# The first layer's MLPs end by halves of tokens, and norms over 256 tokens sum their squares on TensorE

## The chip, the cores and the metric

The kernel runs on one core of one Trainium2 chip. The metric is device time in microseconds (us): 2271.27 us is the median of three runs of the kernel before. One further execution was profiled; all rows below come from it.

## The reference, cut to what matters

Two layers over 1024 tokens of 1024 features. Each layer has a mixer (a state-space mixer in the first, attention over selected keys in the second) and then an MLP, and each of the two is wrapped in norms on both sides:

```python
def rms_norm(x, g):
    y = x * rsqrt(mean(x * x, axis=-1, keepdims=True) + 1e-6)
    return y * g

for i in range(2):
    mix = (s5_mixer, dsa_mixer)[i](rms_norm(h, norm_g[i, 0]), ...)
    h = h + rms_norm(mix, norm_g[i, 1])
    ff = relu(rms_norm(h, norm_g[i, 2]) @ w1[i]) ** 2 @ w2[i]     # 1024 -> 4096 -> 1024
    h = h + rms_norm(ff, norm_g[i, 3])
```

Everything is float32. The change is about the end of the MLP of layer 0: its second product, the norm behind it with the residual sum (gain 3 of the kernel), and the norm ahead of the attention of layer 1 (gain 4).

## The kernel before, in words

The tokens are worked in two halves of 512. Features lie on partitions: an activation of one half is four blocks `[128, 2, 512]` (eight parts of 128 features). To keep float32 accuracy each operand of a large product is split into a high and a low part, and `mm3` (L159 to L161) issues three matmuls for one product, each with 128x128 weights and 512 moving columns. The low parts of weights are made by VectorE and GpSimd (L143), the high ones by ScalarE (L142).

`mlp` has 16 `pair`s of units of `w1` and eight steps `c` of `w2`. In a step four units `d` are loaded, and for each unit and each `j` twelve matmuls fill one PSUM tile `m` that VectorE adds to the accumulator `acc` (L341). With `finish` given, the last step is worked otherwise: its four units are kept (tag `wl`), run first for the tokens 0 to 255 and then for 256 to 511 (matmuls with 256 moving columns, VectorE's sum at L326), and `finish` is called after each half. Only the very last MLP of the program (layer 1, second half) does so before the change.

A norm needs, for each token, the sum of squares over eight parts of 128 features. `squares` has ScalarE square the parts (L186 to L189), an engine add them up (VectorE in the norms of this case, L193), and TensorE reduce over the partitions: for 128 tokens at a time the sum of the parts is the weights and a single column of ones is what moves (L196, output `c`, 128x1; the profile counts two for each such float32 matmul). `post_norm` then forms the reciprocal root on VectorE and ScalarE (L234, `rsqrt` at L167 to L171), spreads it over the partitions with transposes on TensorE (L238), copies it (L240, `rb`), multiplies (L252) and adds the residual (L262). `pre_norm` with gain 4 scales and splits its input into the attention's `x1`, and forms its own squares. `att_r` turns the result into tables for the rotation; its transposes on TensorE are L1179, which wait for copies on ScalarE (L1177).

`run` strings this together: MLP of layer 0 over half 0, `post_norm`, store, `pre_norm`, `att_r`; MLP of layer 0 over half 1, with index, projections and the first attention work of half 0 beside it (the generator `first`); then `att_in(0)`, the same two norms over half 1, `att_r(1)`, and the attention's output product and `index(1)`; later layer 1's MLPs. Within these limits a scheduler sets the order in which each engine gets its instructions: behind a norm that waits, TensorE has matmuls of the next stage in the queue, in the order the scheduler wrote.

## Time and profile before

| what | value |
|---|---|
| median of three runs (lowest, highest) | 2271.27 us (2270.70, 2272.05) |
| the profiled execution: its time | 2264.73 us |
| the profiled execution: its span | 2262.6 us |
| mean granted clock of TensorE | 0.978 of full speed |
| TensorE busy | 2153.9 us, 95% of the span |
| VectorE, ScalarE, GpSimd busy | 1428.8, 1083.2 and 706.5 us |

The span runs from the first to the last instruction on the core; the 2.1 us between it and the execution's time lie around the program. The medians' runs were made apart from the profiled one, which was 6.5 us shorter than their median. "Granted clock" is the share of its full speed (2.4 GHz) that TensorE was given in a stretch; 0.50 is the lower of two levels, 1.2 GHz.

### The profile page before, as it was taken

The page shows a single profiled execution, that of the slowest core. Times are in us where ns is not written, and L with a number is a line of the kernel's source. Part 1 is how long each engine was busy: PE and PEld are TensorE (multiplying, and loading weights), DVE is VectorE, ACT ScalarE, POOL GpSimd, SP SyncE. Part 2 cuts the span into 40 slices and gives each one's busy share as a digit, 9 for nine tenths or more (in the row PEclk, how much of TensorE's full clock was granted, in tenths as well). Part 3 has the DMA queues.
Part 4 walks back from the last instruction along what each step waited for, and adds up shares of the span by engine and source line. Part 5 has one row for each costly group of instructions (what it writes and reads, how often), then busy time and mean ns, then how long its engine had stood idle before and what let it go on. Part 6 is the DMA issues. An engine that isn't in the chain of part 4 may idle for free.

```text
span 2262.6 us, 29481 instructions
## 1 busy us (share of the span) xinstructions
PE 2153.9 (95%) x10376; PEld 1778.6 (79%) x10376; DVE 1428.8 (63%) x2756; ACT 1083.2 (48%) x2024; POOL 706.5 (31%) x593
## 2 busy tenths in 40 slices
PE   8998999999989999999988988999999899999997
PEld 4677788888878888888867866888788687888886
DVE  8667943333745687555686889998767477333335
ACT  5436633333543575555463555787456353333332
POOL 1114632222346423222347533222311135222222
PEclk9999999999999999999999999999999999999998
DMA  7113432333437653445446533334222434423231
GB/s 292 30 32 124 160 111 96 100 94 102 131 105 208 154 132 107 117 107 163 143 146 174 163 102 103 96 82 101 79 81 74 144 137 154 147 84 111 85 112 38
DMA packets 115892, 266.81 MB, mean 118 GB/s; under 512 B 14240, under 2 KB 49568, under 8 KB 115744
## 3 DMA queue, kind: packets, MB, share of 16 engines
q1 hardware_dynamic: 101840, 240.77, 33.3%
q0 software_dynamic: 12672, 23.07, 5.4%
q8 instruction: 82, 1.34, 0.3%
q10 hardware_dynamic: 1232, 1.08, 0.1%
q14 instruction: 66, 0.54, 0.1%
HBM read 229.02 MB, written 34.67 MB: 117 GB/s over the span
## 4 chain that ended last, share of the span: by engine, by line
PE 73%; DVE 14%; ACT 5%; issue 5%; POOL 1%; DMA 1%; SPq 0%; DVEq 0%; ACTq 0%; POOLq 0%
PE m L159 17%; PE m L160 17%; PE m L161 17%; PE m L636 2%; PE p L159 2%; PE p L161 2%; PE p L160 2%; PE p L1082 2%; PE p L1062 2%; DVE wh L143 1%; DVE b L252 1%; PE p L1091 1%; PE p L1090 1%; DVE b L209 1%; ACT junk L1000 1%
## 5 line engine op out<-in xcount | busy, mean ns | idle before, releaser
L159 PE MATMUL m<-b,wh 128*128 128x512 f32 (+1 forms) x2208 | 859.9, 392 | 25.0 <-DVE acc L341 11.0
L160 PE MATMUL m<-b,wh 128*128 128x512 f32 (+1 forms) x2208 | 856.6, 390 | 5.1 <-DVE b L209 4.7
L161 PE MATMUL m<-b,wh 128*128 128x512 f32 (+1 forms) x2208 | 855.0, 390 | 4.3 <-DVE wh L143 4.3
L143 POOL TENSOR_TENSOR wh<-wr,wh 128x512 fp32r<-128x512 f32 (+1 forms) x342 | 440.8, 1294 | 1223.7 <-ACT wh L142 1139.8
L142 ACT ACTIVATE wh<-wr 128x512 fp32r<-128x512 f32 (+1 forms) x684 | 395.3, 592 | 502.7 <-PE m L161 416.2
L159 PEld LDWEIGHTS m<-b,wh 128*128 128x128 f32 x2208 | 418.4, 190 | 113.1 <-DVE acc L341 11.6
L161 PEld LDWEIGHTS m<-b,wh 128*128 128x128 f32 x2208 | 418.5, 190 | 89.3 <-DVE wh L143 5.1
L160 PEld LDWEIGHTS m<-b,wh 128*128 128x128 f32 x2208 | 418.8, 190 | 88.3 <-DVE b L209 6.0
L143 DVE TENSOR_TENSOR wh<-wr,wh 128x512 fp32r<-128x512 f32 (+1 forms) x342 | 266.6, 787 | 294.3 <-ACT wh L142 284.1
L341 DVE TENSOR_TENSOR acc<-acc,m 128x512 f32<-128x512 f32 x216 | 147.1, 682 | 154.0 <-PE m L161 152.3
L306 ACT ACTIVATE b<-m 128x512 f32<-128x512 f32 x128 | 76.2, 595 | 163.6 <-PE m L161 160.6
L150 DVE CAST b<-b 128x1024 fp32r<-128x1024 f32 x68 | 58.1, 854 | 126.8 <-ACT b L308 120.5
L161 PE MATMUL p<-b,wh 128*128 128x512 f32 (+1 forms) x304 | 114.6, 387 | 6.7 <-DVE wh L143 6.7
L159 PE MATMUL p<-b,wh 128*128 128x512 f32 (+1 forms) x304 | 112.9, 388 | 3.2 <-ACT b L747 3.2
L160 PE MATMUL p<-b,wh 128*128 128x512 f32 (+1 forms) x304 | 115.9, 386 | 0.0
L1086 ACT ACTIVATE pt<-p 128x512 fp32r<-128x512 f32 (+1 forms) x160 | 83.6, 553 | 65.6 <-PE p L1082 63.2
L1087 DVE TENSOR_TENSOR pt<-p,pt 128x512 fp32r<-128x512 f32 (+1 forms) x160 | 99.0, 630 | 24.5 <-ACT pt L1086 24.3
L1069 ACT ACTIVATE s<-s,ring 128x128 f32<-128x128 f32 (+7 forms) x128 | 98.5, 772 | 31.7 <-DVE ring L1066 31.3
L1000 ACT ACTIVATE junk<-b,ring 128x512 bf16<-128x512 f32 (+2 forms) x90 | 80.6, 896 | 58.4 <-DVE ring L996 51.8
L1062 PE MATMUL p<-kt,q 128*128 128x512 f32 (+2 forms) x384 | 98.5, 363 | 0.0
L1082 PE MATMUL p<-con,s 128*128 128x128 f32 x576 | 93.8, 272 | 0.8 <-DVE ring L1066 0.7
L1066 DVE CUSTOM_DVE_ANT_0 s<-p,nb 128x512 f32<-128x512 f32 (+3 forms) x128 | 72.6, 583 | 32.8 <-PE p L1062 26.7
(314 smaller groups left out, 2738.8 us busy)
## 6 DMA issues: line engine op xcount, KB each, us to landing
wr<-in_w_dram SPq DMA_DIRECT2D x256, 512.0 KB, 3.7
wr<-in_wa_dram SPq DMA_DIRECT2D x32, 512.0 KB, 3.7
q<-qd POOLq DMA_DIRECT2D x64, 256.0 KB, 5.5
ld<-hd SPq DMA_DIRECT2D x24, 512.0 KB, 6.1
hd<-b SPq DMA_DIRECT2D x16, 512.0 KB, 4.6
qd<-b SPq DMA_DIRECT2D x128, 64.0 KB, 2.0
wr<-in_wao_dram SPq DMA_DIRECT2D x16, 512.0 KB, 3.7
q<-qi POOLq DMA_DIRECT2D x24, 256.0 KB, 4.6
```

Source lines behind the costliest of these rows:

```text
L142: nc.scalar.activation(ph, pr, AF.Copy)
L143: (nc.gpsimd if h else nc.vector).tensor_sub(pl, pr, ph.bitcast(F32))
L159: mm(ps, w[0], x[0], start=start, stop=False)
L160: mm(ps, w[0], x[1], start=False, stop=False)
L161: return mm(ps, w[1], x[0], start=False, stop=stop)
L341: nc.vector.tensor_add(acc[d][:, j], acc[d][:, j], ps)
L1000: nc.scalar.activation(junk[:, 1, :W[j]], keys[j].bitcast(F32), AF.Sign, bias=neg[:, j:j + 1], accum_out=cnt[:, j:j + 1])
L1062: nc.tensor.matmul(ps[:, :m], qt[:, v, 2 * hp + k, :], self.K[c][g // 2][:, g % 2, :m], start=v == 0, stop=v == 1)
L1069: nc.scalar.activation(s, s, AF.Exp, bias=least, scale=-1.0, accum_out=self.sums[:, h:h + 1])
L1082: nc.tensor.transpose(pt[:, kk, k, :], P[k][:, (k0 + kk) * 128:(k0 + kk + 1) * 128], self.ident)
L1086: nc.scalar.activation(ph[:, :nk], pt[:, :nk], AF.Copy)
L1087: nc.vector.tensor_sub(pl[:, :nk], pt[:, :nk], ph.bitcast(F32)[:, :nk])
```

## The change

Two things change. `squares` has a second form, used wherever a norm runs over 256 tokens: ScalarE squares each of the eight parts by itself, nothing is added on VectorE, and TensorE accumulates all eight parts in PSUM, eight matmuls with one moving column for each 128 tokens instead of one. And both MLPs of layer 0 get a `finish`: their last step runs by halves of 256 tokens, and after each half the residual is loaded, `post_norm` runs, the result is stored, and `pre_norm` writes its part of `x1` and of `r`. The work beside the MLP is drained ahead of the last step, and `att_in(0)` is called when the first half of the second MLP is done. Norms over 256 tokens are those of the very last MLP too, so these change in their squares alone.

```diff
--- before.py
+++ after.py
@@ -178,7 +178,22 @@
 
     def squares(self, blocks, add):
 
         nc = self.nc
+        if add is None:
+            n = blocks[0].shape[-1] // 128
+            sqs = []
+            for j, b in enumerate(blocks):
+                sq = self.blk([128, 2, 512], tag=self.scratch_tag)[:, :, :128 * n]
+                for q in range(2):
+                    nc.scalar.activation(sq[:, q], b[:, q], AF.Square)
+                    sqs.append(sq[:, q])
+            ps = self.pc()
+            for k, sq in enumerate(sqs):
+                for t in range(n):
+                    nc.tensor.matmul(ps[:, t:t + 1], sq[:, t * 128:(t + 1) * 128], self.ones,
+                                     start=k == 0 and t == 0, stop=k == 7 and t == n - 1)
+            return ps[:, :n]
         acc, n = None, blocks[0].shape[-1]
         for j, b in enumerate(blocks):
             sq = self.blk([128, 2, 512], tag=self.scratch_tag)[:, :, :n]
@@ -196,26 +211,27 @@
             nc.tensor.matmul(ps[:, j:j + 1], acc[:, j * 128:(j + 1) * 128], self.ones, start=True, stop=True)
         return ps[:, :n // 128]
 
-    def pre_norm(self, h, gi, tag="b", square=True):
+    def pre_norm(self, h, gi, tag="b", square=True, into=None):
 
 
         nc = self.nc
         out = []
         for j, b in enumerate(h):
-            hi, lo = [self.blk([128, 2, 512], F32R, tag=tag) for _ in range(2)]
+            hi, lo = into[0][j] if into else [self.blk([128, 2, 512], F32R, tag=tag) for _ in range(2)]
             for q in range(2):
                 g = self.gain[:, gi, 2 * j + q:2 * j + q + 1]
                 nc.scalar.activation(hi[:, q], b[:, q], AF.Copy, scale=g)
                 nc.vector.scalar_tensor_tensor(lo[:, q], b[:, q], g, hi.bitcast(F32)[:, q],
                                                op0=ALU.mult, op1=ALU.subtract)
             out.append((hi, lo))
-        s = self.squares(h, nc.gpsimd.tensor_add if square else nc.vector.tensor_add)
-        r = self.small([128, 4], F32, "kept")
+        s = self.squares(h, None if into else nc.gpsimd.tensor_add if square else nc.vector.tensor_add)
+        r = into[1] if into else self.small([128, 4], F32, "kept")
         nc.vector.tensor_scalar(r, s, 1.0 / 1024, EPS, op0=ALU.mult, op1=ALU.add)
         if square:
             nc.vector.scalar_tensor_tensor(r, r, 1024 * EPS, r, op0=ALU.mult, op1=ALU.mult)
         else:
-            nc.vector.tensor_copy(r, self.rsqrt(r, 4)[:, :4])
+            n = r.shape[-1]
+            nc.vector.tensor_copy(r, self.rsqrt(r, n)[:, :n])
         return out, r
 
     def post_norm(self, f, gi, h, e=None, reorder=False, last=None, aside=False):
@@ -223,8 +239,8 @@
 
 
         nc = self.nc
-        s = self.squares(f, nc.vector.tensor_add)
         n = f[0].shape[-1]
+        s = self.squares(f, nc.vector.tensor_add if n == 512 else None)
         m = n // 128
         ms = self.small([128, 4], F32)
         if e is None:
@@ -314,6 +330,8 @@
             while len(hid) < min(2 * c + 3 + (c >= 6), 16):
                 pair(len(hid))
             if finish and c == 7:
+                for _ in side or ():
+                    pass
                 ws = [self.unit(w2[L, c, d], last=True) for d in range(4)]
                 for th in range(2):
                     n = slice(256 * th, 256 * th + 256)
@@ -1253,9 +1271,32 @@
             self.store_h(dst[hf], h)
             return h
 
+        def halves(hf, first=lambda: None):
+
+
+            x = [tuple(self.blk([128, 2, 512], F32R) for _ in range(2)) for _ in range(4)]
+            r = self.small([128, 4], F32, "kept")
+
+            def take(n, f):
+                if not n.start:
+                    first()
+                m = slice(n.start // 128, n.stop // 128)
+
+                def load(j):
+                    t = self.blk([128, 2, 512], name="ld", tag="ld")[:, :, :256]
+                    self.nc.sync.dma_start(t, hd[0][hf][j][:, :, n])
+                    return t
+
+                h = self.post_norm(f, 3, [lambda j=j: load(j) for j in range(4)], xn[hf][1][:, m])
+                for j in range(4):
+                    self.nc.sync.dma_start(hd[1][hf][j][:, :, n], h[j])
+                self.pre_norm(h, 4, square=False, into=([[t[:, :, n] for t in b] for b in x], r[:, m]))
+
+            return take, x, r
+
         self.nc.sync.dma_start(self.rope, a["rope"])
-        acc = self.mlp(0, xn[0][0])
-        x1, r = self.pre_norm(residual(0, acc, 3, hd[0], hd[1], xn[0][1]), 4, square=False)
+        take, x1, r = halves(0)
+        self.mlp(0, xn[0][0], finish=take)
         self.att_r(0, r)
         self.att_start()
 
@@ -1264,9 +1305,11 @@
             yield from self.projections(0, x1)
             yield from self.attention_a()
 
-        acc = self.mlp(0, xn[1][0], first(), PER_A, WAIT_A)
-        xo = finished(self.att_in(0, "x"))
-        x1, r = self.pre_norm(residual(1, acc, 3, hd[0], hd[1], xn[1][1]), 4, square=False)
+        side = first()
+        xo = []
+        take, xb, r = halves(1, lambda: xo.extend(finished(self.att_in(0, "x"))))
+        self.mlp(0, xn[1][0], side, PER_A, WAIT_A, finish=take)
+        x1 = xb
         self.att_r(1, r)
         for _ in self.att_out(xo, "hid"):
             pass
```

The change moves instructions on TensorE at three places. First, TensorE at the end of the first MLP. `m_530` to `m_570` are tiles of the second MLP's first product, `c_492` (before) is the sum of squares of the post-norm over 512 tokens, `c_516` (after) that of the pre-norm over tokens 0 to 255 and `c_532` that of the post-norm over tokens 256 to 511. Before, one of the two places with one-column matmuls reads:

```order
L159 MATMUL m_530_4299<-b262_1730,wh529_0_4293 128x512
L160 MATMUL m_530_4299<-b263_1731,wh529_0_4293 128x512
L196 MATMUL c_492_4134<-con_72,b488_4118 128x1 x4
L161 MATMUL m_530_4299<-b262_1730,wh529_0_4293 128x512
L159 MATMUL m_530_4299<-b264_1736,wh529_0_4293 128x512
```

and of the change, the longest such row of that place:

```order
L160 MATMUL m_568_4515<-b269_1749,wh567_1_4512 128x512
L194 MATMUL c_516_4218<-con_72,b512_4206 128x1 x4
L194 MATMUL c_516_4218<-con_72,b513_4209 128x1 x4
L194 MATMUL c_516_4218<-con_72,b514_4212 128x1 x4
L194 MATMUL c_516_4218<-con_72,b515_4215 128x1 x4
L194 MATMUL c_532_4366<-con_72,b528_4354 128x1 x4
L194 MATMUL c_532_4366<-con_72,b529_4357 128x1 x4
L194 MATMUL c_532_4366<-con_72,b530_4360 128x1 x4
L194 MATMUL c_532_4366<-con_72,b531_4363 128x1 x4
L161 MATMUL m_568_4515<-b268_1748,wh567_1_4512 128x512
```

Four one-column matmuls stood between two wide ones; now 32 stand there in a row. Two further groups of 16 stand behind the first half of tokens (broken by a single wide matmul) and at the end of the place, and the end of the second MLP has the same three groups.

Second, TensorE at the transposes of `att_r` (`p1_521` and `p1_523` before, `p1_552` after) a little later. Before:

```order
L159 MATMUL m_558_4575<-b538_4400,wh555_1_4557 128x512
L160 MATMUL m_558_4575<-b539_4401,wh555_1_4557 128x512
L161 MATMUL m_558_4575<-b538_4400,wh555_1_4557 128x512
L1179 MATMUL p1_521_4231<-con_72,b522_4232 128x128 x4
L1179 MATMUL p1_523_4239<-con_72,b524_4240 128x128
L159 MATMUL p1_560_4597<-b503_4176,wh559_0_4591 128x512
```

After the change:

```order
L159 MATMUL m_582_4663<-b268_1748,wh581_1_4660 128x512
L160 MATMUL m_582_4663<-b269_1749,wh581_1_4660 128x512
L1197 MATMUL p1_552_4473<-con_72,b553_4474 128x128 x4
L161 MATMUL m_582_4663<-b268_1748,wh581_1_4660 128x512
L159 MATMUL m_584_4697<-b262_1730,wh583_0_4691 128x512
```

The two groups of transposes were adjacent; now the first stands among wide matmuls, and the second group further behind.

Third, TensorE at the end of the program (`m_3116` before, `m_3178` after: the last tile of the last product). Before:

```order
L160 MATMUL m_3116_18785<-b3073_18338,wh3089_1_18514 128x256
L161 MATMUL m_3116_18785<-b3072_18337,wh3089_1_18514 128x256
L196 MATMUL c_3121_18815<-con_72,b3117_18799 128x1 x2
L238 MATMUL c_3126_18824<-con_72,ring_73 128x128 x2
L1381 UNCONDITIONAL_BRANCH
```

After the change:

```order
L161 MATMUL m_3178_19279<-b3134_18821,wh3151_1_18998 128x256
L194 MATMUL c_3183_19305<-con_72,b3179_19293 128x1 x4
L194 MATMUL c_3183_19305<-con_72,b3180_19296 128x1 x4
L194 MATMUL c_3183_19305<-con_72,b3181_19299 128x1 x4
L194 MATMUL c_3183_19305<-con_72,b3182_19302 128x1 x4
L254 MATMUL c_3188_19328<-con_72,ring_73 128x128 x2
```

Sixteen one-column matmuls have taken the place of two behind the last wide one. Apart from the ends of the three MLPs TensorE's order is unchanged.

## Rows read from the trace of the kernel before

**Rows 1.** This is the page: the span's line, and TensorE's line of busy time (us, share of the span, number of instructions); and from its DMA issues the loads of the residual (number, KB each, median us from issue to landing).

```profile
span 2262.6 us, 29481 instructions
...
PE 2153.9 (95%) x10376; PEld 1778.6 (79%) x10376; DVE 1428.8 (63%) x2756; ACT 1083.2 (48%) x2024; POOL 706.5 (31%) x593
...
ld<-hd SPq DMA_DIRECT2D x24, 512.0 KB, 6.1
```

**Rows 2.** This is the timeline of TensorE around 588 us, in the middle of a stretch of 512-column matmuls; columns as in the next groups too: start us, duration us, engine, line, operation, output <- inputs, shape of the moving operand and type, how many, and in brackets idle time before and what ended it. `128x1` is the matmul with one moving column.

```profile
588.06 0.39 PE L160 MATMUL m<-b,wh 128*128 128x512 f32 x1
588.29 0.95 PE L196 MATMUL c<-con,b 128*128 128x1 f32 x8
589.09 0.49 PE L161 MATMUL m<-b,wh 128*128 128x512 f32 x1
589.42 0.40 PE L159 MATMUL m<-b,wh 128*128 128x512 f32 x1
```

**Rows 3.** This is the timeline of TensorE: two 512-column matmuls that are twelve apart in an undisturbed row, and two 256-column matmuls that are twelve apart in the last MLP.

```profile
622.12 0.39 PE L160 MATMUL m<-b,wh 128*128 128x512 f32 x1
...
624.84 0.39 PE L160 MATMUL m<-b,wh 128*128 128x512 f32 x1
...
2239.06 0.28 PE L159 MATMUL m<-b,wh 128*128 128x256 f32 x1
...
2240.50 0.28 PE L159 MATMUL m<-b,wh 128*128 128x256 f32 x1
```

**Rows 4.** This is the waits of TensorE at the end of the first MLP (620 to 650 us; engine, line waited for, us in total, times, longest), and its timeline there.

```profile
PE c L196 <- DVE b L193: 3.8, 1, 3.8
PE p L1179 <- ACT b L1177: 1.9, 1, 1.9
...
630.18 1.84 PE L196 MATMUL c<-con,b 128*128 128x1 f32 x8 [3.82 <-DVE b L193]
```

**Rows 5.** This is busy time by stretch at the same place: from:to us, its length, busy us and (number) of PE, PEld, DVE, ACT and POOL, the granted clock of TensorE, DMA share, GB/s.

```profile
626.00:630.20 4.20, 0.38 (x3) 0.05 (x1) 4.06 (x6) 1.31 (x4) 1.49 (x1) 0.80 0.42 125
630.20:635.35 5.15, 5.15 (x16) 4.47 (x17) 4.67 (x12) 1.49 (x5) 1.42 (x2) 0.50 0.34 105
...
640.10:642.10 2.00, 0.08 (x2) 0.07 (x2) 0.00 (x0) 1.88 (x5) 1.40 (x2) 1.00 0.00 0
642.10:645.55 3.45, 3.45 (x9) 2.80 (x10) 0.00 (x0) 0.00 (x0) 0.00 (x0) 0.51 0.48 152
```

**Rows 6.** This is the waits of TensorE at the end of the second MLP of the first layer (1099 to 1160 us), and its timeline at the first of them.

```profile
PE p L1179 <- ACT b L1177: 2.9, 2, 1.4
PE c L196 <- DVE b L193: 2.0, 1, 2.0
...
1141.54 1.02 PE L196 MATMUL c<-con,b 128*128 128x1 f32 x8 [2.04 <-DVE b L193]
```

**Rows 7.** This is busy time by stretch at that place; columns as in rows 5.

```profile
1139.50:1141.50 2.00, 0.01 (x1) 0.00 (x0) 1.79 (x4) 2.00 (x6) 0.12 (x1) 1.00 0.53 121
1141.50:1143.90 2.40, 2.36 (x14) 2.13 (x15) 2.30 (x3) 2.40 (x7) 1.87 (x2) 1.00 0.29 118
1143.90:1147.30 3.40, 3.40 (x9) 2.65 (x8) 3.37 (x6) 0.52 (x2) 2.12 (x2) 0.50 0.50 152
...
1149.10:1153.10 4.00, 1.11 (x10) 0.88 (x9) 1.49 (x6) 3.25 (x8) 1.41 (x2) 1.00 0.10 39
```

**Rows 8.** This is busy time by stretch at two places of the first mixer, where TensorE runs matmuls with 16 and with 128 moving columns (95.6 and 120.6 us) and 512-column ones behind the second (127.4 us), and at a wait of 1.84 us in a later stage (871.8 us); columns as in rows 5.

```profile
95.60:101.80 6.20, 6.20 (x31) 6.20 (x32) 4.64 (x6) 1.59 (x3) 0.00 (x0) 0.53 0.10 28
...
120.60:127.40 6.80, 6.78 (x31) 6.39 (x32) 5.20 (x6) 0.99 (x2) 0.00 (x0) 0.50 0.00 0
127.40:130.20 2.80, 2.80 (x9) 2.23 (x9) 0.74 (x1) 2.51 (x4) 0.00 (x0) 0.51 0.23 64
...
874.25:877.65 3.40, 3.40 (x10) 2.66 (x9) 3.40 (x9) 0.00 (x0) 1.01 (x1) 0.50 0.33 98
```

**Rows 9.** This is the timeline of TensorE and of VectorE at the end of the program: last wide matmul and squares' matmuls; then VectorE's chain for the reciprocal root, behind the first half of the tokens (2236.52 to 2237.90) and behind the second, and its products and sums.

```profile
2243.82 0.28 PE L161 MATMUL m<-b,wh 128*128 128x256 f32 x1
2246.56 1.01 PE L196 MATMUL c<-con,b 128*128 128x1 f32 x4 [2.46 <-DVE b L193]
...
2236.52 0.16 DVE L234 TENSOR_TENSOR ring<-c,con 128x2 f32<-128x2 f32 x1
...
2237.90 0.16 DVE L171 SCALAR_TENSOR_TENSOR ring<-ring 128x2 f32<-128x2 f32 x1
...
2247.61 0.16 DVE L234 TENSOR_TENSOR ring<-c,con 128x2 f32<-128x2 f32 x1 [1.11 <-PE c L196]
...
2249.18 0.65 DVE L171 SCALAR_TENSOR_TENSOR ring<-ring 128x2 f32<-128x2 f32 x1
2251.09 4.75 DVE L252 SCALAR_TENSOR_TENSOR acc<-acc,con,rb 128x256 f32<-128x256 f32 x8 [1.26 <-ACT rb L240]
2255.76 2.76 DVE L262 TENSOR_TENSOR acc<-acc,ld 128x256 f32<-128x256 f32 x8
```

**Rows 10.** This is busy time by stretch at the end of the program; columns as in rows 5.

```profile
2247.60:2250.00 2.40, 0.03 (x1) 0.06 (x2) 1.84 (x5) 0.20 (x1) 2.40 (x5) 0.50 0.00 0
...
2251.10:2262.60 11.50, 0.00 (x0) 0.00 (x0) 7.41 (x16) 0.00 (x0) 2.47 (x4) 0.50 0.48 163
```

## The prediction

> **What bounds the kernel now.** The page comes first: TensorE is busy for 95% of the span and no other engine for more than 63% [rows 1]. So a microsecond of work put into TensorE's row costs a microsecond unless the row was waiting there, and work taken from VectorE is worth only what TensorE waits for it. I therefore went through TensorE's idle time and its granted clock at the three places where its order changes.
>
> At the end of the first MLP the waits name two things [rows 4]: the one-column matmuls wait 3.82 us for VectorE's sum of squares, and the transposes of `att_r` 1.9 us for a copy on ScalarE. The clock falls to 0.50 with the first wait and to 0.51 with the second, and stays there for 5.15 us and 3.45 us of busy time [rows 5]. At full clock wide matmuls start 0.227 us apart ((624.84 - 622.12) / 12 [rows 3]); at half clock half of the time is lost: 2.6 and 1.7 us. Together 3.8 + 1.9 + 2.6 + 1.7 = 10.0 us.
>
> At the end of the second MLP the same waits are 2.0 and 2.9 us [rows 6], and one low stretch of 3.40 us costs 1.7 us [rows 7]: 6.6 us. At the end of the program [rows 9] nothing runs beside the chain: the last wide matmul starts at 2243.82, the squares' matmuls at 2246.56 after 2.46 us of waiting, VectorE's chain for the root runs from 2247.61 to 2249.83 and the products and sums from 2251.09 to 2258.52.
>
> **The change part by part.** All terms are made against the profiled execution, 2264.7 us; the sum is then laid on the median, 2271.3 us, which stands 6.5 us above it.
>
> *One-column matmuls.* The row at 588 us gives their price inside a busy stretch [rows 2]. The L160 at 588.06 is followed by four of them (eight in the profile's count) and one L161; undisturbed, the L159 would start two spacings after it, at 588.51. It starts at 589.42: 0.91 us for four, 0.227 us each. Nothing hides this, since TensorE was full before and behind. The squares of 512 tokens took 4 per norm; two norms of 256 take 2 x 16. Two norms at each MLP end make 64 instead of 8: 56 x 0.227 = 12.7 us per MLP end. At the program's end 16 for the first half instead of 2 cost 14 x 0.227 = 3.2 us in the busy row; the last 16 run mostly while squares are still being made.
>
> *Narrower matmuls.* The last step has four units of two tiles of twelve: 96 matmuls of 512 columns become 192 of 256. These start 0.120 us apart (1.44 us for twelve [rows 3]), so 96 x (2 x 0.120 - 0.227) = +1.3 us per MLP end.
>
> *The waits that go.* With halves, the first half's norms lie beside the second half's matmuls, and the second half's post-norm has `m` tiles of the next MLP (first place) or `att_in(0)` (second place) in the queue. ScalarE's squares of a part need no sum on VectorE behind them, and the adjacent transposes are apart. What may be late next is the eighth square on ScalarE, whose matmul stands ahead of wide ones in TensorE's queue; I keep 1 us of waits at each place. Gain: 10.0 - 1 = 9.0 and 6.6 - 1 = 5.6 us. The bounds are the whole gain on one side and a wait as long as the old one on the other (rival 2).
>
> *Transfers and order.* The residual now comes in eight loads instead of four at each end, and the result leaves in eight stores, all on SP's queue among the weights' loads. A load there took 6.1 us from issue to landing [rows 1], and the first half's norms have the second half's matmuls beside them (96 x 0.120 = 11.5 us), so I cost them at nothing; without that cover a late load would delay the residual sum, and through it `x1` and the projections. The work beside the second MLP is drained ahead of its last step and `att_in(0)` called within it, but TensorE's order away from the three ends is what it was, so this costs nothing either.
>
> *The end of the program.* VectorE's chain takes 2.2 us behind the second half but only 1.5 us behind the first (2236.52 to 2238.06 [rows 9]); GpSimd was busy for all of the 2.40 us around the slow one [rows 10]. With the sums gone the chain and the products (4.75 + 2.76 us) meet less of it: I take -0.7 for the chain and -1.3 for products and sums; ends of this estimate: 0 and -3. With 0.1 for small things the place is 3.2 + 0.1 - 2.0 = +1.3 us.
>
> Sum at a full clock: (12.7 + 1.3 - 9.0) + (12.7 + 1.3 - 5.6) + 1.3 = 5.0 + 8.4 + 1.3 = **+14.7 us**.
>
> *The clock.* The groups of one-column matmuls are long: 16 take 3.6 us, 32 take 7.3 us. No row of before shows one so long, so the cost has two ends. Below it is nothing, if TensorE's being busy is enough. The rows speak against that: at 95.6 us TensorE was busy for all of 6.20 us with matmuls of few columns at a clock of 0.53, at 120.6 us for 6.78 of 6.80 at 0.50, and the clock came back only after 2.8 us of 512-column matmuls [rows 8]. And at 1139.5 us a wait of 2.04 us and eight one-column passes together were followed by a low clock [rows 6, 7], where the transposes' waits of up to 1.4 us (1149 us) were not. Above, the clock falls soon after a group begins, and a one-column pass then takes twice as long (eight in 1.84 us at 630.18 against 0.95 at 588.29 [rows 2, 4]). For the 32 I let the clock fall after 2 to 4 us: the remaining 3.3 to 5.3 us double, and the 3.4 us of wide matmuls at half clock behind them [rows 7, 8] lose 1.7: 5.0 to 7.0, taken as 5.5 us. The 16 fall only late in the group or not at all: 0 to 3.5, taken as 2 us each. Per MLP end 2 + 5.5 + 2 = 9.5 us, twice 19; at the program's end 2 us for its first group. Clock: **+21.0 us**, nearest to the rows of 95.6 and 120.6 us.
>
> For the clock's other end there is a page: the Trainium skill, "TensorE: Matmul & The Clock Gate", section "Why this matters for your kernels", has it that the clock is lost through idle gaps between bursts of matmuls. By that alone the groups cost nothing for the clock, and the sum would be +14.7 us. The rows at 95.6 us do not settle this, because they show a clock that does not rise, not one that falls in busy time.
>
> Total: 14.7 + 21.0 = +35.7 us: 2264.7 + 35.7 = 2300.4 us profiled, and 2271.3 + 35.7 = **2307 us** for the median.
>
> **The rivals.**
> 1. *The clock holds.* Long one-column groups count as work for the clock like wide ones. Then 2271.3 + 14.7 = 2286 us. For it: no row shows a fall without a wait ahead. Against: the low clock through busy stretches of small matmuls.
> 2. *The waits stay.* ScalarE makes 16 squares of 256 tokens for each half's two norms, besides the splits of weights (L142). If it is behind, TensorE waits at the groups as long as it did for VectorE, 3.8 and 2.0 us, and for transposes 1.9 and 2.9: 10.6 us in all, 2 of which are in the sum: 2307 + 8.6 = 2316 us.
> 3. *The passes are cheap (the other sign).* At one place, the norms' groups: were the one-column matmuls hidden behind wide ones, 126 of them (56 + 56 + 14) would cost none of their 28.6 us, the clock would have no long stretch to fall in, and 14.7 - 28.6 = -13.9 gives 2257 us. It becomes a gain when a matmul costs under 0.227 - 14.7 / 126 = 0.110 us. Against it: 0.227 in the row at 588 us. The Trainium skill, same page, section "Back-to-back issue gap", gives a floor of about 25 ns between starts at few columns; by it 252 passes would take 6.3 us, and the sum would be -7.6 us. The trace disagrees: 0.113 us per pass, with a fresh weight load for each.
> 4. *No change to speak of.* The gains at the ends are larger than counted and meet the passes' price: within 0.2%, which is 4.5 us and about what a measurement of this kernel can tell from no change.
>
> **How the numbers follow.** Chances: forecast 0.68, rival 1 0.15, rival 2 0.09, rival 3 0.05, rival 4 0.03. The forecast's own range is 2295 to 2315 (groups of 16 at 0 to 3.5 us, of 32 at 5 to 7, the end of the program). The range reaches down past rival 1's 2286 by the ends of the program's-end estimate, to 2283, and up past rival 2 with the upper end of the clock's cost, to 2322; outside remain rivals 3 and 4 and some of the tails. Faster by over 0.2%: 0.05; within: 0.03; slower: 0.92.
>
> **What the changed profile would show.** One-column matmuls on TensorE (L194): 160 of them where the forecast's groups stand, groups of 16 and 32 in a row at 0.113 us per pass where the clock holds and 0.23 where it fell. The granted clock at 0.5 inside the group of 32 and behind it, at both MLP ends. The waits for L193 gone and those for L1177's copy shorter. 256-column matmuls 0.120 us apart. An unchanged length of everything between the three places. I am wrong if the clock is 1.00 through the groups (rival 1), if `c` waits for ScalarE for more than 2 us at a place (rival 2), or if the passes take under 0.06 us each in a full row (rival 3).

## The result, and the profile after

The changed kernel takes 2294.61 us (median of four runs, 2293.89 to 2296.41) against 2271.66 us for the kernel before, a ratio of 1.0103 with a 95% interval of [1.0084, 1.0122]: it is 1% slower. A second measurement beside the last experiments gave 2294.32 us and 1.0105 [1.0085, 1.0125]. The forecast was 2307 us with a range of 2283 to 2322, so the direction and the range held, though 2294.61 us lies just under the forecast's own narrower range of 2295 to 2315; the size, +35.7 us, was 1.6 times the +23 us measured.

The page of the changed kernel's profiled execution, which took 2295.24 us:

```profile
span 2293.4 us, 30593 instructions
...
PE 2206.4 (96%) x10848; PEld 1837.8 (80%) x10848; DVE 1406.4 (61%) x2788; ACT 1093.2 (48%) x2096; POOL 698.7 (30%) x597
```

TensorE is busier by 52.5 us and the span is longer by 30.8 us than in [rows 1]: the added matmuls went onto the path, and the waits that they replaced were shorter than they are. Where the 30.8 us came from is read by cutting both executions at the same instructions. In these views of busy time by stretch the columns are those of [rows 5]. Before:

```profile
0.00:560.00 560.00, 531.94 (x2441) 416.83 (x2442) 314.44 (x556) 238.49 (x374) 156.19 (x115) 0.98 0.34 114
560.00:672.00 112.00, 105.35 (x508) 88.58 (x507) 65.40 (x97) 54.01 (x100) 38.57 (x35) 0.95 0.36 111
672.00:1075.00 403.00, 400.24 (x1997) 338.92 (x1996) 264.88 (x632) 215.17 (x487) 142.14 (x142) 1.00 0.54 142
1075.00:1158.00 83.00, 78.08 (x350) 64.03 (x349) 57.37 (x83) 42.69 (x72) 26.26 (x18) 0.98 0.45 152
1158.00:2158.00 1000.00, 950.48 (x4610) 793.82 (x4609) 677.92 (x1305) 501.15 (x937) 313.56 (x256) 0.98 0.38 114
2158.00:2262.60 104.60, 87.77 (x480) 76.39 (x478) 48.76 (x87) 31.73 (x57) 29.84 (x29) 0.92 0.19 66
```

And of the changed kernel, cut at the same matmuls:

```profile
0.00:562.80 562.80, 537.02 (x2441) 421.03 (x2442) 317.20 (x560) 242.67 (x382) 158.48 (x119) 0.97 0.35 115
562.80:686.90 124.10, 124.10 (x716) 111.50 (x715) 53.04 (x116) 53.98 (x126) 32.42 (x33) 0.92 0.30 94
686.90:1088.30 401.40, 398.65 (x1995) 337.42 (x1995) 266.41 (x629) 216.32 (x490) 143.82 (x143) 1.00 0.56 143
1088.30:1187.70 99.40, 99.40 (x559) 89.32 (x558) 51.10 (x108) 45.49 (x102) 22.65 (x18) 0.90 0.39 125
1187.70:2188.30 1000.60, 953.91 (x4609) 796.31 (x4609) 678.74 (x1305) 501.44 (x937) 312.48 (x256) 0.98 0.38 114
2188.30:2293.40 105.10, 93.36 (x536) 82.18 (x534) 39.96 (x73) 33.26 (x63) 28.83 (x29) 0.94 0.19 66
```

The second stretch (end of the first MLP) grew from 112.0 to 124.1 us, the fourth (end of the second MLP) from 83.0 to 99.4 us, and the last (end of the program) from 104.6 to 105.1 us: +12.1, +16.4 and +0.5. The other three, whose instructions stand in the same order, changed by +2.8, -1.6 and +0.6 us. (The cuts meet to within two matmuls, which can move 0.3 us from the fourth stretch to the third.) In the second and fourth stretch TensorE is now busy for the whole of 124.10 and 99.40 us, where it had been idle for 6.65 and 4.92 us. All waits are gone there. What replaced them stands in the clock column, 0.92 and 0.90 instead of 0.95 and 0.98.

The groups of one-column matmuls at the end of the first MLP, busy time by stretch, cut where the clock changes:

```profile
574.30:577.90 3.60, 3.60 (x36) 3.60 (x34) 0.42 (x1) 0.42 (x1) 0.00 (x0) 1.00 0.00 0
577.90:581.30 3.40, 3.40 (x18) 3.40 (x18) 1.23 (x6) 0.20 (x1) 0.00 (x0) 0.50 0.01 2
...
595.60:598.40 2.80, 2.80 (x27) 2.76 (x26) 0.25 (x1) 2.52 (x8) 0.00 (x0) 1.00 0.03 10
598.40:606.80 8.40, 8.40 (x41) 8.40 (x41) 1.42 (x7) 0.20 (x1) 0.00 (x0) 0.50 0.01 2
606.80:612.10 5.30, 5.30 (x13) 4.14 (x14) 0.81 (x5) 1.32 (x3) 1.28 (x1) 0.51 0.00 0
...
625.40:629.10 3.70, 3.70 (x34) 3.70 (x33) 3.70 (x6) 2.24 (x6) 1.58 (x1) 1.00 0.61 184
629.10:632.50 3.40, 3.40 (x9) 2.61 (x9) 2.17 (x10) 1.05 (x3) 0.00 (x0) 0.50 0.28 112
```

A group of 16 matmuls, broken by one wide matmul, fills 574.3 to 578.0 us; the clock falls at its very end, and TensorE runs at half clock for 3.40 us. The group of 32 begins at 595.6; 2.80 us into it the clock falls to 0.50, and stays there for the other 8.40 us of the group and for 5.30 us of wide matmuls behind. The last group (625.4) is again followed by 3.40 us. TensorE is busy in each of these stretches for their whole length, so no wait stands ahead of any of the falls. Half of 3.40 + 8.40 + 5.30 + 3.40 us is 10.25 us lost. The low stretches of the second MLP's end:

```profile
1106.95:1110.35 3.40, 3.40 (x18) 3.40 (x17) 0.80 (x4) 0.00 (x0) 0.00 (x0) 0.50 0.00 0
...
1127.50:1134.50 7.00, 7.00 (x35) 7.00 (x35) 0.97 (x6) 0.20 (x1) 0.00 (x0) 0.50 0.00 0
1134.50:1137.70 3.20, 3.20 (x8) 2.52 (x9) 0.80 (x5) 1.32 (x3) 0.44 (x1) 0.50 0.00 0
...
1154.75:1161.60 6.85, 6.85 (x22) 5.79 (x22) 2.79 (x11) 3.35 (x7) 1.28 (x1) 0.50 0.64 248
```

Half of 3.40 + 7.00 + 3.20 + 6.85 us is 10.2 us. The end of the program, TensorE's last group and VectorE's work behind it:

```profile
2277.35 3.63 PE L194 MATMUL c<-con,b 128*128 128x1 f32 x32
...
2281.01 0.16 DVE L250 TENSOR_TENSOR ring<-c,con 128x2 f32<-128x2 f32 x1 [3.05 <-PE c L194]
...
2282.03 0.16 DVE L171 SCALAR_TENSOR_TENSOR ring<-ring 128x2 f32<-128x2 f32 x1
2283.39 3.26 DVE L268 SCALAR_TENSOR_TENSOR acc<-acc,con,rb 128x256 f32<-128x256 f32 x8 [1.20 <-ACT rb L256]
2286.56 2.77 DVE L278 TENSOR_TENSOR acc<-acc,ld 128x256 f32<-128x256 f32 x8
```

The chain for the root takes 1.18 us (2281.01 to 2282.19) where it took 2.22 us, and products and sums 5.94 us (2283.39 to 2289.33) where they took 7.43 us [rows 9].

### The profile page after: what moved, and what is told of

It reads as the page before. It is cut to its first block, busy times and chain, and to the rows that moved or that the text cites. A ratio compares the mean times of both kernels' runs of the same rounds, so it can differ in the third digit from the quotient of the medians.

```text
span 2293.4 us, 30593 instructions
## 1 busy us (share of the span) xinstructions
PE 2206.4 (96%) x10848; PEld 1837.8 (80%) x10848; DVE 1406.4 (61%) x2788; ACT 1093.2 (48%) x2096; POOL 698.7 (30%) x597
## 4 chain that ended last, share of the span: by engine, by line
PE 76%; DVE 11%; ACT 4%; issue 4%; POOL 3%; DMA 2%; SPq 0%; DVEq 0%; POOLq 0%; ACTq 0%
PE m L160 18%; PE m L159 18%; PE m L161 18%; PE m L654 2%; PE p L1100 2%; PE p L1080 2%; PE p L159 2%; PE p L160 2%; PE p L161 2%; PE c L194 2%; DVE b L268 1%; PE p L1109 1%; PE p L1108 1%; ACT junk L1018 1%; DVE wh L143 1%
## 5 line engine op out<-in xcount | busy, mean ns | idle before, releaser
L159 PE MATMUL m<-b,wh 128*128 128x512 f32 (+1 forms) x2272 | 876.3, 388 | 22.1 <-DVE acc L359 9.8
L160 PE MATMUL m<-b,wh 128*128 128x512 f32 (+1 forms) x2272 | 872.8, 386 | 4.4 <-DVE b L224 3.9
L161 PE MATMUL m<-b,wh 128*128 128x512 f32 (+1 forms) x2272 | 871.1, 386 | 4.3 <-DVE wh L143 4.3
L143 POOL TENSOR_TENSOR wh<-wr,wh 128x512 fp32r<-128x512 f32 (+1 forms) x342 | 435.8, 1279 | 1214.0 <-ACT wh L142 1106.5
L159 PEld LDWEIGHTS m<-b,wh 128*128 128x128 f32 x2272 | 434.6, 191 | 108.9 <-DVE acc L359 11.6
L161 PEld LDWEIGHTS m<-b,wh 128*128 128x128 f32 x2272 | 434.2, 191 | 87.3 <-DVE wh L143 5.2
L160 PEld LDWEIGHTS m<-b,wh 128*128 128x128 f32 x2272 | 434.8, 191 | 85.2 <-DVE b L224 4.8
L143 DVE TENSOR_TENSOR wh<-wr,wh 128x512 fp32r<-128x512 f32 (+1 forms) x342 | 270.6, 799 | 331.3 <-ACT wh L142 321.3
L359 DVE TENSOR_TENSOR acc<-acc,m 128x512 f32<-128x512 f32 x200 | 135.9, 682 | 135.7 <-PE m L161 134.5
```

What stands on the lines that cost most here:

```text
L143: (nc.gpsimd if h else nc.vector).tensor_sub(pl, pr, ph.bitcast(F32))
L159: mm(ps, w[0], x[0], start=start, stop=False)
L160: mm(ps, w[0], x[1], start=False, stop=False)
L161: return mm(ps, w[1], x[0], start=False, stop=stop)
L359: nc.vector.tensor_add(acc[d][:, j], acc[d][:, j], ps)
```

## The experiments

Three theories stood against each other. **Theory:** the time is the price of the one-column matmuls, 0.227 us each, plus the clock that is lost in and behind their long groups. **Rival one:** the halves of tokens cost it (narrower matmuls, more norms). **Rival two:** it is waits, of TensorE for ScalarE or VectorE.

**Each part of the change alone.** First the halves with VectorE's sums:

```diff
-        s = self.squares(h, None if into else nc.gpsimd.tensor_add if square else nc.vector.tensor_add)
+        s = self.squares(h, nc.gpsimd.tensor_add if square else nc.vector.tensor_add)
...
-        s = self.squares(f, nc.vector.tensor_add if n == 512 else None)
+        s = self.squares(f, nc.vector.tensor_add)
```

> Both first-layer MLPs end by halves of tokens, as in the change, but the squares of 256-token norms are added on VectorE as before, so that TensorE has 2 one-column matmuls per norm. Theory (the one-column matmuls cost the time, 0.227 us each and in addition the clock that falls in their long groups): without their 28.6 us and without some 20 us of clock the halves alone remain, with the two MLP ends' waits gone: about 10 us under the kernel before, and no low clock at the two ends. Rival (the halves cost the time: narrower matmuls, twice as many norms): 10 us or more over the kernel before, low clock still there. Second rival (VectorE's sums make TensorE wait again): waits of TensorE for VectorE of 2 us or more at each end, and a time within 5 us of before.

Measured: 2267.31 us, ratio to before 0.9987 [0.9970, 1.0005], no change that can be told. The halves are not what costs. The waits of TensorE at the first and at the second MLP's end:

```profile
PE p L1197 <- ACT b L1195: 2.1, 1, 2.1
...
PE p L161 <- DVE wh L143: 8.8, 1, 8.8
PE p L1197 <- ACT b L1195: 5.3, 2, 4.1
PE c L254 <- DVE ring L171: 2.1, 1, 2.1
PE c L211 <- DVE b L208: 1.6, 1, 1.6
```

The first end went as the theory said: 2.8 us of waits where there were 6.65, no low clock, and 6.7 us shorter than before. At the second, waits are back: 1.6 us for VectorE's sum of squares (L208) and 5.3 us for ScalarE's copies (L1195), with 6.8 us of low clock behind the longest of them, and the place grew by 4 us. The waits of 2.1 us (the root of a later norm) and of 8.8 us (weights' low parts on VectorE, L143) stand behind the place, where the scheduler wrote another order of the attention's work than in before and after. So the expected -10 us was only in part to be had. The time is the one that the second rival named, within 5 us of before, but its wait, 2 us or more for VectorE's sums at each end, did not come: the longer wait is for ScalarE.

Then the kernel before with the second form of `squares` added, and used for the old ends over 512 tokens, four groups of 32:

```diff
-        s = self.squares(h, nc.gpsimd.tensor_add if square else nc.vector.tensor_add)
+        s = self.squares(h, nc.gpsimd.tensor_add if square else None)
...
-        s = self.squares(f, nc.vector.tensor_add)
...
+        s = self.squares(f, None if gi == 3 else nc.vector.tensor_add)
```

> The MLPs end as before, over 512 tokens, but the four norms behind the first layer's MLPs have their squares accumulated on TensorE, 32 one-column matmuls in a row each; the last MLP's norms are as before. Theory: 4 x 28 x 0.227 = 25.4 us for the matmuls, some 5 us of clock for each group of 32, less up to 6 us of waits for VectorE's sums and some low clock behind these: 30 to 40 us over the kernel before, the clock at 0.50 inside each group after about 3 us. Rival (the halves cost the time): within 5 us of the kernel before, or faster, since VectorE is relieved.

Measured: 2287.91 us, 1.0083 [1.0070, 1.0095], +17 us; the sign is the theory's, the size was set too high. Two of the four groups, by stretch:

```profile
585.50:588.50 3.00, 3.00 (x29) 3.00 (x28) 0.32 (x1) 0.95 (x2) 1.27 (x1) 1.00 0.18 26
588.50:598.90 10.40, 10.40 (x42) 9.63 (x42) 0.82 (x5) 0.21 (x1) 0.00 (x0) 0.51 0.12 43
1111.00:1114.30 3.30, 3.30 (x31) 3.30 (x31) 0.00 (x0) 1.39 (x2) 0.79 (x1) 0.99 0.42 108
1114.30:1124.50 10.20, 10.20 (x36) 8.95 (x37) 0.83 (x5) 0.34 (x2) 0.00 (x0) 0.50 0.04 17
```

The rows begin inside their groups. From its first one-column matmul on, each of the four groups kept the full clock for 3.3 to 5.1 us and then lost it for some 10 us, as in the changed kernel. The expectation forgot that the groups replace waits with a low clock of their own: before lost 10.0 and 6.6 us at these places. 25.4 us for the matmuls plus 4 x 5.1 us of clock less 16.6 is +29; by the traces, cut at the same instructions, the two ends grew by 10.9 and 14.7 us, 25.6 together. That is against the profiled execution of before; its median stands 6 us higher, which is most of what separates 25.6 from the +17 us of the medians.

**The clock by itself.** The same matmuls, each with 128 columns of ones:

```diff
-                    nc.tensor.matmul(ps[:, t:t + 1], sq[:, t * 128:(t + 1) * 128], self.ones,
+                    nc.tensor.matmul(ps[:, t * 128:(t + 1) * 128], sq[:, t * 128:(t + 1) * 128],
+                                     self.ones.to_broadcast([128, 128]),
...
-            return ps[:, :n]
+            return ps[:, 0:128 * n:128]
```

> The changed kernel, but each of the square matmuls moves 128 columns of ones instead of one, so that each result stands 128 times; their number, order and weights are the same. Theory (a group with one moving column loses the clock): the clock stays at 1.00 through the groups or falls later, a pass takes 0.113 to 0.14 us (eight 128-column passes took 1.09 us elsewhere in the trace of before), and the time is 10 to 20 us under the changed kernel. Rival (the clock falls because of something else, such as waits or the halves): the same low clock, and a time equal to the changed kernel's or up to 8 us over it.

Measured: 2280.02 us, 14 us under the changed kernel; ratio to before 1.0041 [1.0028, 1.0054]. The groups by stretch:

```profile
595.90:603.30 7.40, 7.40 (x66) 7.33 (x65) 1.70 (x8) 3.28 (x10) 1.27 (x1) 1.00 0.26 71
603.30:612.00 8.70, 8.70 (x41) 7.14 (x40) 3.07 (x9) 3.81 (x7) 1.29 (x1) 1.00 0.05 12
622.80:626.70 3.90, 3.90 (x35) 3.82 (x35) 1.81 (x6) 3.90 (x11) 0.43 (x1) 1.00 0.24 83
```

The group of 32 takes 7.4 us at a clock of 1.00, and 1.00 stands behind it and in the groups of 16. A pass with 128 columns takes 7.4 us / 64 = 0.116 us, the same as one with a single column (0.113). The number of square matmuls, their groups and their duration at full clock are equal, so the difference at the ends is the clock. The scheduler moved some wide matmuls and transposes at the ends, so these are best taken together with the stage between them: from the start of the first end to the end of the second the kernel before takes 598.0 us, this kernel 605.4 and the changed kernel 624.9. Of the 19.5 us between these last two, close to the 20.4 us that the low clock cost above, some 6 were given back between 1200 and 1800 us, where this kernel has the same other order of the attention's work as the one with the halves alone.

**The end of the program alone.** The kernel before with the second form of `squares` in the last MLP's two norms:

```diff
-        s = self.squares(f, nc.vector.tensor_add)
...
+        s = self.squares(f, nc.vector.tensor_add if n == 512 else None)
```

> The kernel before, with the squares on TensorE only in the two 256-token norms of the very last MLP. Prediction's term: +1.3 us and 2 us for the clock, so +3 us; the profile of the changed kernel shows about +0.5 us for that place. Rival (VectorE's relief at the end gains more than the matmuls cost): 1 to 3 us under the kernel before. All are within what a measurement can tell; the trace of the end of the program decides: length from the last wide matmul to the end, 18.8 us before.

Measured: 2273.48 us, 1.0010 [1.0000, 1.0020]. The forecast of +3 us is inside the interval, and the rival's gain is outside it. The length from the last wide matmul to the end is 16.2 us instead of 18.8, so the relief that the rival named is there, 2.6 us of it; ahead of it stand the 3.2 us of 14 more matmuls and 1.7 us of clock, and the last stretch grew by 2.0 us. Its first group of 16:

```profile
2239.10:2243.90 4.80, 4.80 (x45) 4.80 (x44) 1.00 (x5) 1.40 (x4) 0.00 (x0) 1.00 0.00 0
2243.90:2247.30 3.40, 3.40 (x18) 3.40 (x18) 0.73 (x4) 0.42 (x1) 0.00 (x0) 0.50 0.00 0
```

Here it was followed by 3.40 us at half clock; in the changed kernel's execution above the same group, at 2262 us, was not. The same instructions can so cost 1.7 us or nothing. This run, whose profiled execution took 2273.80 us against a median of 2270.78 for the kernel before beside it, is also an execution of before in all but its end; cut at the same instructions:

```profile
0.00:563.20 563.20, 537.22 (x2441) 421.36 (x2442) 313.91 (x556) 238.48 (x374) 155.17 (x115) 0.97 0.34 113
563.20:675.80 112.60, 105.93 (x508) 88.91 (x507) 65.42 (x97) 54.04 (x100) 38.46 (x35) 0.95 0.35 111
...
1078.90:1164.20 85.30, 78.75 (x349) 64.62 (x348) 57.40 (x83) 42.72 (x72) 26.27 (x18) 0.96 0.44 148
1164.20:2165.40 1001.20, 953.46 (x4611) 796.41 (x4610) 679.75 (x1305) 500.92 (x937) 312.97 (x256) 0.97 0.37 113
```

Up to the last stretch it is 7.4 us longer than the profiled execution of before: 3.2, 0.6, 0.1, 2.3 and 1.2 us. In the first of these stretches, which no change touches, TensorE was busy for 537.2 us instead of 531.9 at a mean clock of 0.97 instead of 0.98.

**The amount.** First fewer matmuls, with VectorE adding the two parts of each block:

```diff
                 nc.scalar.activation(sq[:, q], b[:, q], AF.Square)
-                    sqs.append(sq[:, q])
+                nc.vector.tensor_add(sq[:, 0], sq[:, 0], sq[:, 1])
+                sqs.append(sq[:, 0])
...
-                                     start=k == 0 and t == 0, stop=k == 7 and t == n - 1)
+                                     start=k == 0 and t == 0, stop=k == 3 and t == n - 1)
```

> The changed kernel, but VectorE adds the two squared parts of each block first (four sums of 128x256 per norm), so that TensorE has 8 instead of 16 one-column matmuls per norm of 256 tokens: groups of 6 to 8, 16 and 8 stand in TensorE's order instead of 16, 32 and 16, and its order behind the first layer is that of the changed kernel and of before. Theory (price per matmul, and the clock lost in long groups): 63 x 0.227 = 14.3 us less for the matmuls, and of about 20 us of clock only 2 to 6 us left, since a group of 16 is at its end when the clock falls: 26 to 32 us under the changed kernel, some 5 us under the kernel before. Rival (the ends cost what they cost by halves and by waits, not by matmuls): 5 us or less under the changed kernel. Second rival (VectorE's sums bring waits back): TensorE waits for VectorE by 2 us or more at each end, and the time is that of the kernel before or over it.

Measured: 2262.85 us, 0.9956 [0.9941, 0.9971], 31.8 us under the changed kernel (26 to 32 were expected) and faster than before. Its middle groups, now of 16, at both ends:

```profile
594.60:598.30 3.70, 3.70 (x34) 3.68 (x33) 2.40 (x5) 2.90 (x7) 1.18 (x1) 1.00 0.01 4
598.30:601.50 3.20, 3.20 (x15) 2.60 (x15) 2.23 (x12) 1.18 (x4) 0.09 (x1) 1.00 0.46 164
...
1111.90:1115.30 3.40, 3.40 (x9) 2.61 (x8) 1.80 (x12) 1.43 (x4) 0.00 (x0) 0.51 0.45 154
```

At the first end the clock holds through 3.70 us and behind; at the second it is at half behind the group for 3.40 us, which costs 1.7. So the sum at the two ends is 56 x 0.227 = 12.7 us of matmuls and 20.4 - 1.7 = 18.7 us of clock, less 1.6 us of new waits: 29.8 us. By the traces, cut at the same instructions, the ends are some 16 and 13 us shorter than the changed kernel's.

With the same pairs and 128 columns of ones:

```diff
-                    nc.tensor.matmul(ps[:, t:t + 1], sq[:, t * 128:(t + 1) * 128], self.ones,
+                    nc.tensor.matmul(ps[:, t * 128:(t + 1) * 128], sq[:, t * 128:(t + 1) * 128],
+                                     self.ones.to_broadcast([128, 128]),
...
-            return ps[:, :n]
+            return ps[:, 0:128 * n:128]
```

> As the run with the pairs added on VectorE, and each of the square matmuls moves 128 columns of ones. Theory: the clock stays at 1.00 through all groups, so up to 5 us under the run with pairs alone in the two ends; but its order behind the first layer (1200 to 1600 us) is that of the run with 128 columns, where the trace shows 6 us lost, so 2264 to 2272 us in all. Rival (128 columns cost more than one): 5 us over the run with pairs alone at the ends themselves.

Measured: 2267.73 us, 0.9978 [0.9962, 0.9995]. That is inside the 2264 to 2272 us expected: where the second end is over it is 3.2 us ahead of the run with pairs, of which the clock, which stayed at 1.00 there, explains 1.7, and it gives that back behind 1200 us, in the other order.

Then twice as many:

```diff
-                    nc.scalar.activation(sq[:, q], b[:, q], AF.Square)
+                    nc.scalar.activation(sq[:, q], b[:, q], AF.Square, scale=0.5 ** 0.5)
...
-            for k, sq in enumerate(sqs):
+            for k, sq in enumerate(s for s in sqs for _ in range(2)):
...
-                                     start=k == 0 and t == 0, stop=k == 7 and t == n - 1)
+                                     start=k == 0 and t == 0, stop=k == 15 and t == n - 1)
```

> The changed kernel with each one-column matmul of the 256-token norms issued twice (the squares are halved on ScalarE, so the sum is the same): groups of 32, 64 and 32. Theory: 126 more matmuls on the path at 0.227 us, 28.6 us at a full clock, and nearly all of the added ones at the low clock, where each takes 0.46 us: with 3 us at full clock per group, a group of 32 takes 11 us and one of 64 some 26 us, so each MLP end grows by 25 to 30 us, and the whole by 50 to 70 us over the changed kernel. Rival (a group costs once, for its waits and for filling the array, not by its length): at most 15 us more.

Measured: 2368.64 us, 1.0417 [1.0385, 1.0449], 74 us over the changed kernel, a little over the theory's upper end. The group of 64:

```profile
604.40:607.30 2.90, 2.90 (x28) 2.90 (x26) 0.69 (x1) 1.96 (x6) 0.00 (x0) 0.98 0.05 16
607.30:629.20 21.90, 21.90 (x104) 21.90 (x104) 1.01 (x7) 0.20 (x1) 0.00 (x0) 0.50 0.00 1
```

It takes 24.8 us (26 expected), 2.9 of them at full clock. The two MLP ends grew by 27.3 and 27.7 us, inside what was expected of them; the end of the program, to which the expectation left little, grew by some 15.

**Fewer still.** The last two kernels were measured beside each other. The first, against the run with pairs:

```diff
+                if j % 2:
+                    nc.vector.tensor_add(sq[:, 0], sqs.pop(), sq[:, 0])
                 sqs.append(sq[:, 0])
...
-                                     start=k == 0 and t == 0, stop=k == 3 and t == n - 1)
+                                     start=k == 0 and t == 0, stop=k == 1 and t == n - 1)
```

> As the run with the pairs added on VectorE, but VectorE adds four parts (six sums of 128x256 per norm), so that TensorE has 4 one-column matmuls per norm, in groups of 2 in its order. By the price per matmul alone: 31 x 0.227 = 7.1 us under the run with pairs, about 2256 us. Rival (TensorE now waits for VectorE's sums again): each end takes back 2 to 5 us in waits for them, with a low clock behind a wait of about 2 us, and the time is 2262 us or more.

Measured: 2253.99 us, 0.9928 [0.9911, 0.9945]: faster than before by 0.7% and the best of all versions. Busy time at its two ends, and its waits at the second:

```profile
560.00:660.00 100.00, 98.80 (x581) 86.75 (x580) 62.88 (x137) 49.58 (x116) 29.62 (x29) 1.00 0.33 108
1056.00:1150.00 94.00, 90.02 (x515) 78.52 (x513) 73.39 (x148) 50.69 (x114) 30.64 (x26) 1.00 0.47 155
...
PE c L257 <- DVE ring L171: 2.1, 1, 2.1
PE c L197 <- DVE b L192: 1.2, 1, 1.2
```

The clock is at 1.00 in both. Waits for VectorE's sums (L192) are back, but with 1.2 us at the second end and 0.4 us at the first they are short, and no fall of the clock follows them within the two stretches. (The wait of 2.1 us is that of a later norm over 512 tokens, at 1148.7 us, behind the end.) The price alone gave 2256 us; the rival's 2262 us did not come.

The other of the two was the changed kernel once more:

> The changed kernel as it is, measured beside the next run and the kernel before on one chip. By the traces the three ends of MLPs grew by 12.1, 16.4 and 0.5 us against the profiled execution of before, and by about 26 us in all against an execution of before with the usual clock elsewhere. Theory (the profiled execution of before had a better clock than usual in stretches that the change does not touch): 22 to 27 us over the median of before. Rival (the growth seen in the traces is the growth of every execution): 29 to 31 us over.

Measured: 2294.32 us against 2272.22, +22.1 us. The theory's side holds, at its lower edge. The profile of this run, cut at the same matmuls, shows the growth of the first execution again at the two first-layer ends (+12.1 and +16.2 us, with 10.2 us lost to the low clock at each), and +2.0 instead of +0.5 us at the end of the program, because this time the clock fell behind the first group of 16 there:

```profile
2264.40:2267.90 3.50, 3.50 (x19) 3.50 (x18) 0.83 (x4) 0.42 (x1) 0.00 (x0) 0.51 0.02 5
```

Both executions of the changed kernel stand about 30 us over the one profiled execution of before (30.8 and 29.9 us of span), so it is that one which is out of line with its median.

## Why the prediction was right in sign and range, and where its size was off

*The price of a one-column matmul* held nearly. The matmuls and the narrower last step were to cost 12.7 + 1.3 = 14.0 us per MLP end. With what was lost to waits and low clock before and after, the runs give 12.1 + 10.9 - 10.25 = 12.8 us at the first end and 16.4 + 6.6 - 10.2 = 12.8 us at the second: the forecast had some 1.2 us too much per end, with the 0.3 us of the cuts to allow for.

*The clock in the long groups* was the step most in doubt, and it held: 9.5 us forecast per end, 10.25 and 10.2 measured. Its parts were spread otherwise: the group of 32 at the first end lost (8.40 + 5.30) / 2 = 6.9 us instead of 5.5, the groups of 16 there 1.7 us each instead of 2. Rival 1 (the clock holds) is refuted by the clock rows of the changed kernel, and the run with 128 columns shows what it would have given. One of the rows that argued against it was misread: the stretch at 120.6 us begins with four 512-column matmuls, 1.9 of its 6.8 us, and both this stretch and the one at 95.6 us stand behind a wait (1.86 and 2.42 us). Every fall in the rows of before stood behind a wait, so this step, though right, went beyond what they showed. The rule of the Trainium skill that stood beside it ("TensorE: Matmul & The Clock Gate", section "Why this matters for your kernels": idle gaps are what costs the clock) gave +14.7 us; this case's trace disagrees, since the clock fell inside groups without any idle time, at 598.4 us and at 1127.5 us. At the end of the program 2 us were counted; none came in the first execution of the changed kernel, and 1.7 us in its second and in the run with that part alone.

*The waits that go* were sized too low. I kept 1 us at each end for a late square on ScalarE; no such wait exists, and the 0.9 us behind the transposes' stage went too: 10.9 us gone instead of 9.0, and 6.6 instead of 5.6. Rival 2 is refuted for the changed kernel.

*The end of the program* was to cost 1.3 us at full clock and cost 0.5: the chain gained 1.0 and products and sums 1.5 us, against the 2.0 us assumed together.

Of the +35.7 us (14.5 + 17.9 + 3.3) the three places thus made +29.0 (12.1 + 16.4 + 0.5) between the two profiled executions. The rest of the miss is *the last step*, where the sum, made against one profiled execution, was laid unaltered on the median 6.5 us above it. That execution was shorter than usual: the one shown above (before in all but its end) lost more to the low clock, partly in stretches that nothing touched, partly at the very ends that the change rebuilt (0.6 and 2.3 us). So the change removed 2.9 us more than the profiled execution let see, and the changed kernel's own execution lost 2.7 us less than that other one in untouched stretches (+2.8 - 1.6 + 0.6 against +3.2 + 0.1 + 1.2): 29.0 - 2.9 - 2.7 = 23.4 us, close to the 22 and 23 us of the medians. This is the difference of two traces, not a check from elsewhere: it says that one execution of before near its median gives the growth of the medians. That the clock makes the difference can be seen in the first stretch, where TensorE's instructions are the same in all eleven traces: in the two with 23.9 us at half clock, the profiled execution of before among them, it took 559.0 and 560.2 us, and in the four with 37.6 us, among them both of the changed kernel and the one shown above, 562.9 to 564.8. For the other stretches it stays likely rather than shown.

Two of the prediction's bounds do not follow from its own terms. With five groups of 16 at 3.5 us, two of 32 at 7.0 and no gain at the end of the program, the forecast's own range would end at about 2319, not 2315; and the outer range, by the same terms, would be about 2285 to 2326 instead of 2283 to 2322. The measured time lies inside either outer range.

Rival 3 (cheap passes) is refuted by the price, and rival 4 by the result.

## What to carry to other kernels

Moving a sum from an engine with slack to the engine that bounds the kernel pays only for as much as the bound engine waits for it; here 4 matmuls per norm instead of 16, with six sums left on VectorE, turned +1.0% into -0.7%. Long runs of matmuls with a single moving column had a second price here beside their duration, because the clock fell in each group of 32 and more though TensorE never stood idle: look at a group's length, not only at the number of its instructions. No run kept the number and broke the groups up, so what that alone would give is not shown. If a group must stay, 128 columns of ones cost the same time per pass and kept the clock; in both kernels with them, though, the scheduler also wrote another order of the attention's work, which cost some 4 to 6 us. Before a forecast is laid on a median, compare the profiled execution with the other runs, and look for low-clock stretches that it lacks.

## What the runs showed of the hardware that I had not expected

One and 128 moving columns take the same time with fresh float32 weights each (0.113 and 0.116 us per pass), yet the clock fell to 0.50 inside each of the 16 groups of 32 and more of the first kind, 2.2 to 5.1 us after the group's start and with TensorE busy throughout, and in none of the second, of which the longest took 7.4 us. With a group of 16 the low stretch began late in the group or up to 1.1 us behind it and was mostly 3.4 us long, in one place 6.85 us; in two places none came. At the end of the program, one of these two, it came in one execution of the changed kernel and not in the other, with the same instructions in the same order.
